# A gate matrix product taken half as seven block products for eight, half plain

## The chip, the cores and the metric

The kernel runs on one NeuronCore of one Trainium2 chip, as one launch. The metric is the device time of the launch in microseconds: 2138.77 us is the median of three runs (2138.43, 2138.77 and 2140.12). Engines are named as in the profile: PE multiplies matrices (TensorE), PEld is its weight load, DVE is VectorE, ACT is ScalarE, POOL is GpSimd, and SP only issues transfers (DMA) between device memory (DRAM) and the on-chip memory SBUF. Matrix products land in a second on-chip memory, PSUM.

## The reference

One layer on 1024 tokens of 2048 channels, all in float32. Only its last part matters here; what comes ahead is unchanged.

```python
hn = rms_norm(h, norm_mix)                     # 2048 channels
q, k, v, gate_a, u, gate_s = split(hn @ w_in)  # attention and SSM groups
y_attn = block_attention(q, k, v) * silu(gate_a)          # 1024 channels
y_ssm = gelu(s5_bidirectional(u, ...))
glu = y_ssm @ w_glu + b_glu
y_ssm = glu[..., :1024] * sigmoid(glu[..., 1024:]) * silu(gate_s)
h = h + concatenate([y_attn, y_ssm]) @ w_out   # 2048 x 2048
gate = sigmoid(rms_norm(h, norm_ple) @ w_ple_gate)        # 2048 x 2048
h = h + gate * (p @ w_ple_proj)                # p has 256 channels
return rms_norm(h, norm_final)
```

## The kernel before

Activations lie with the channel on the 128 partitions and the token on the free axis, so a "k-tile" is 128 input channels and a row tile is 128 output channels; 1024 tokens are two halves of 512. A product keeps float32 accuracy by splitting both operands into a high part H (rounded to `fp32r`) and a rest L, and by three matmuls: H·H, H·L, L·H. A split costs one ACT instruction (the cast, line 310 or 313) and one DVE instruction (the subtraction, line 311 or 314).

The back part of the kernel (function `back`) first runs three product stages of eight units each: stage 0 is `w_glu`, stage 1 the attention half of `w_out`, stage 2 the SSM half of `w_out`. A unit makes two row tiles over all 1024 tokens from eight k-tiles as a 2 by 2 by 2 block product, and needs seven block products for eight (Strassen's scheme in Winograd's form). Each of the seven has 4 k-tiles by 3 matmuls of 128x512, so a unit has 84 matmuls (lines 1183 to 1185). The sums of weight blocks are made as the unit nears (`sw_sum`, on POOL, for units 18 to 22 on DVE); the sums of activation blocks are made once for a stage by `t_make` on POOL and kept in DRAM (`d_t`). The results are combined on DVE as each product leaves PSUM; in `u_out` POOL adds partial results into the residual tile `cx`, and a delayed DVE addition (`close`, line 1273) closes a quarter of it. Stage 2 also squares the new h on ACT and adds up the squares on POOL (line 1285) for the next norm.

The 28 split activation tiles `X` of a stage (7 products by 4 k-tiles, tiles `st`) serve all eight units. They are loaded and split during the last unit of the stage ahead, as their buffers come free: `put` issues the load on SP, `fill` splits the tile some ticks later. A tick comes after every third matmul of a product, and in the product stages fills are left out in one tick of five. With `share=True` every seventh fill is split on POOL instead (lines 318 and 319), 4 of the 28.

The gate stage (`gate`) goes plainly over the two token halves: for each half and each of 16 row tiles it takes all 16 k-tiles of `w_gate` and 2 of `w_proj`, 54 matmuls of 128x512 (lines 1322 to 1324). Its weights pass through three raw buffers (`wraw`), loaded by SP and split on ACT and DVE two tiles ahead of use. `fin_g` scales the gate product by the token's reciprocal root (`xsq`), applies the sigmoid on ACT, multiplies by the second product on DVE, and adds `h` on POOL, which also adds up squares for the final norm. `finish` of the first half (16 DVE instructions, line 1392, and 16 output stores) runs beside the second half.

The order of the work on each engine is the order in which this program is written, with background generators (`bg`) stepped once per tick; each engine, and each DMA queue, works through its own list in order and waits where an operand is not there.

Of the kernel before, what the change touches and what calls it, by code (L numbers as in the profile page):

```python
# [238 lines left out]
class Kernel:  # L239
# [269 lines left out]
    def scratch(self):  # L509
# [15 lines left out]
        self.d_t = [[d(f"d_t{s}_{k}", (2, 128, SEQ)) for k in range(4)] for s in range(3)]  # L525
# [597 lines left out]
    def t_make(self, s, src, four, k_wait, lag):  # L1123

        gp = self.nc.gpsimd

# [185 lines left out]
    def mm_half(self, ps, nk, xs, each=None):  # L1312

        nc = self.nc
        for k in range(nk):
# [9 lines left out]
            if k % 2:  # L1325
                self.tick()
                if each:
                    each(k)

    def h_rstd(self):  # L1330
        for _ in range(3):
            yield
# [4 lines left out]
        for _ in range(4):  # L1337
            yield
# [3 lines left out]
    def fin_g(self, hf, n, pg, pp, ho, hp, acc):  # L1342
# [72 lines left out]
    def put_h(self, hg, hf, ks, wait=4):  # L1415
        for k in ks:
            self.put(hg, k, self.d_h[k][:, self.half(hf)], self.g_ple[:, k : k + 1], wait=wait)

    def gate(self, hf, hg, nhg):
        nc = self.nc  # L1420
        sl = self.half(hf)
        hs, pT = [], {}
        acc = self.t2k(("zz", "t4")[hf])
        self.bg(self.p_load(hf, pT))
        for n in range(16):
# [3 lines left out]
            ho = self.bk.tile([128, 512], F32, name="cx", tag="cx", bufs=4)  # L1429
            nc.sync.dma_start(ho, self.d_h[n][:, sl])  # L1430
            if hf == 0 and n == 0:
                self.bg(self.h_rstd())
            if hf == 0 and 12 <= n < 15:
                self.put_h(nhg, 1, range(3 * n - 36, 3 * n - 33))
            if hf == 0 and n == 15:
                self.mm_half(pg, 16, hg, lambda k: k < 15 and self.put_h(nhg, 1, [9 + k // 2], wait=3))
            else:
                self.mm_half(pg, 16, hg)
# [3 lines left out]
            self.bg(self.fin_g(hf, n, pg, pp, ho, hs[n], acc))  # L1442
        if hf == 1:
            self.drain()
        self.bg(self.finish(hf, hs, acc))

    def back(self, X):
# [8 lines left out]
        units = [(s, u, stages[s][1](u)) for s in range(3) for u in range(8)]
        next(units[0][2])
        nX = {}
        for n, (s, u, thread) in enumerate(units):

            def hook(i):
                if n == 0 and i == 0:
                    self.put_product(X, 6, 0, self.d_y2)
                if u < 7:
                    if u == 6 and i == 6:
                        if s < 2:
                            self.put_product(nX, 0, s + 1, stages[s + 1][0])
# [4 lines left out]
                elif s < 2:
                    if i < 6:
                        self.put_product(nX, i + 1, s + 1, stages[s + 1][0], wait=8, share=True)
                else:
                    if i < 2:
                        if i == 1:
                            self.w_dma()
                            self.w_dma()
                        self.put_h(hg, 0, range(5 + 4 * i, 9 + 4 * i), wait=8)  # L1480
                    elif i == 2:
                        self.put_h(hg, 0, [13], wait=8)
# [12 lines left out]
        self.put_h(hg, 0, [14, 15], wait=3)
        nhg = {}
        self.gate(0, hg, nhg)
        self.gate(1, nhg, None)
# [199 lines left out]
```

## Time and profile before

| | |
|---|---|
| median of three runs | 2138.77 us |
| the profiled execution | 2137.65 us, its span 2135.8 us |
| product stages 0 to 2, first to last matmul | 1227.2 to 1703.9 us |
| gate stage, first to last gate matmul | 1704.6 to 2111.6 us |
| after it, to the end of the span | about 24 us |
| busy share of the span: PE, DVE, ACT, POOL | 97%, 69%, 42%, 43% |

A PE instruction of 128x512 is shown as 0.39 us long, but they are pipelined and overlap, so a busy PE says little; the starts of the matmuls say how fast they pass. Where a table by stretches gives "(x61)", that is the number of instructions that started in the stretch, and with the regular distance between two matmuls it tells how much of the stretch PE lost.

### The profile page before, as it was taken

What the parts mean: (1) busy time and instruction counts of PE and PEld (TensorE: products, weight loads), DVE (VectorE), ACT (ScalarE), POOL (GpSimd) and SP (SyncE); (2) the same over time, 40 slices, a digit from 0 to 9 for tenths busy, and PEclk for the clock granted to TensorE, in tenths of its full rate; (3) what the DMA queues carried; (4) which work ended last, traced back from release to release, by engine and by line L of the source; (5) the groups of instructions that cost most, each with busy time, mean ns of one, the idle gap of its engine ahead of it and who ended that gap; (6) DMA issues with size and microseconds to landing.
All of it is one profiled execution on the core that took longest, in us unless ns stands there. A gap on an engine that the chain in (4) does not pass through costs nothing.

```text
span 2135.8 us, 29630 instructions
## 1 busy us (share of the span) xinstructions
PE 2062.8 (97%) x10140; PEld 1716.9 (80%) x10140; DVE 1469.1 (69%) x2406; ACT 897.7 (42%) x1614; POOL 919.1 (43%) x833
## 2 busy tenths in 40 slices
PE   8999999999999999998999999989999999999996
PEld 6888878888887878887889878878878778888885
DVE  7654787778888787847998976764677743456433
ACT  7111322222222222346777765654565643343332
POOL 0143465555656554613320556477565621221122
PEclk9999999999999999999999999999999999999998
DMA  6333224233233233454421366668765544455433
GB/s 217 91 103 103 78 75 119 74 90 99 83 85 114 73 95 89 148 171 148 159 70 50 128 227 221 217 197 284 250 205 172 176 139 129 130 183 171 150 110 128
DMA packets 183126, 296.50 MB, mean 139 GB/s; under 512 B 28352, under 2 KB 78656, under 8 KB 182720
## 3 DMA queue, kind: packets, MB, share of 16 engines
q1 hardware_dynamic: 181824, 292.51, 43.0%
q10 hardware_dynamic: 1152, 2.10, 0.3%
q8 instruction: 81, 1.33, 0.3%
q14 instruction: 69, 0.57, 0.1%
HBM read 211.37 MB, written 77.92 MB: 135 GB/s over the span
## 4 chain that ended last, share of the span: by engine, by line
PE 54%; DVE 9%; DMA 3%; ACT 2%; issue 1%; POOL 1%; SPq 1%; DVEq 0%; ACTq 0%; POOLq 0%
PE pr L1183 6%; PE pr L1184 6%; PE pr L1185 6%; PE pg L1322 5%; PE pg L1323 5%; PE pg L1324 5%; PE ptr L1015 2%; PE zgs L579 2%; PE zgs L582 2%; PE zgs L580 2%; DMA st<-d_t 1%; PE pv L1029 1%; PE pv L1028 1%; PE pv L1030 1%; PE S L985 1%
## 5 line engine op out<-in xcount | busy, mean ns | idle before, releaser
L311 DVE TENSOR_TENSOR wL<-wraw,wH 128x512 fp32r<-128x512 f32 x304 | 253.5, 852 | 297.5 <-ACT wH L310 294.0
L310 ACT CAST wH<-wraw 128x512 fp32r<-128x512 f32 x304 | 175.5, 595 | 264.5 <-DMA wraw<-in_w_gate_dram 98.5
L1183 PE MATMUL pr<-st,wH 128*128 128x512 f32 x672 | 264.2, 393 | 12.1 <-DVE cx L1273 7.1
L1185 PE MATMUL pr<-st,wL 128*128 128x512 f32 x672 | 263.8, 393 | 0.0
L1184 PE MATMUL pr<-st,wH 128*128 128x512 f32 x672 | 263.4, 392 | 0.2 <-DVE st L311 0.2
L1324 PE MATMUL pg<-st,wL 128*128 128x512 f32 x512 | 200.2, 391 | 3.6 <-DVE wL L311 3.6
L1322 PE MATMUL pg<-st,wH 128*128 128x512 f32 x512 | 200.9, 392 | 1.0 <-ACT wH L310 1.0
L1323 PE MATMUL pg<-st,wH 128*128 128x512 f32 x512 | 200.3, 391 | 0.5 <-DVE st L314 0.5
L1352 POOL TENSOR_TENSOR h<-cx,tz 128x512 f32<-128x512 f32 x31 | 40.9, 1321 | 292.6 <-DVE tz L1350 292.6
L1183 PEld LDWEIGHTS pr<-st,wH 128*128 128x128 f32 x672 | 127.3, 189 | 41.3 <-ACT hp L450 5.8
L897 ACT COPY ks<-kp 16x224 f32<-16x224 f32 x32 | 10.7, 336 | 342.3 <-DVE ks L896 229.3
L1185 PEld LDWEIGHTS pr<-st,wL 128*128 128x128 f32 x672 | 127.3, 189 | 27.7 <-DVE wL L451 0.9
L1184 PEld LDWEIGHTS pr<-st,wH 128*128 128x128 f32 x672 | 127.4, 190 | 26.9 <-DVE st L311 0.6
L1324 PEld LDWEIGHTS pg<-st,wL 128*128 128x128 f32 x512 | 96.5, 188 | 24.8 <-DVE wL L311 4.5
L1322 PEld LDWEIGHTS pg<-st,wH 128*128 128x128 f32 x512 | 96.5, 188 | 23.4 <-ACT wH L310 1.8
L449 ACT CAST wH<-sraw 128x512 fp32r<-128x512 f32 x120 | 74.3, 619 | 96.4 <-PE pr L1184 77.6
L1265 POOL TENSOR_TENSOR cx<-cx,tz 128x512 f32<-128x512 f32 x64 | 87.8, 1384 | 61.1 <-DVE tz L1297 40.7
L1323 PEld LDWEIGHTS pg<-st,wH 128*128 128x128 f32 x512 | 96.5, 188 | 21.5 <-DVE st L314 1.3
L451 DVE TENSOR_TENSOR wL<-sraw,hp 128x512 fp32r<-128x512 f32 x120 | 81.9, 683 | 42.3 <-ACT hp L450 36.4
L770 POOL TENSOR_TENSOR tab<-pa 128x512 f32<-128x512 f32 x32 | 41.4, 1293 | 157.8 <-DVE r L905 157.8
L579 PE MATMUL zga<-hH,wH 128*128 128x512 f32 x256 | 104.0, 406 | 0.0
L579 PE MATMUL zq<-hH,wH 128*128 128x512 f32 x256 | 103.3, 404 | 0.0
(377 smaller groups left out, 5556.5 us busy)
## 6 DMA issues: line engine op xcount, KB each, us to landing
wraw<-in_w_in_dram SPq DMA_DIRECT2D x144, 256.0 KB
wraw<-in_w_gate_dram SPq DMA_DIRECT2D x128, 256.0 KB
sraw<-in_w_out_dram SPq DMA_DIRECT2D x64, 256.0 KB
st<-d_t SPq DMA_DIRECT2D x48, 256.0 KB
sraw<-in_w_glu_dram SPq DMA_DIRECT2D x32, 256.0 KB
cx<-in_xT_dram SPq DMA_DIRECT2D x16, 512.0 KB
d_p<-cx SPq DMA_DIRECT2D x16, 512.0 KB
cx<-d_p SPq DMA_DIRECT2D x16, 512.0 KB
```

The lines of the kernel that those rows point to most:

```text
L310: nc.scalar.copy(H, src)
L311: nc.vector.tensor_tensor(L, src, H.bitcast(F32), ALU.subtract)
L449: self.nc.scalar.copy(H, raw)
L451: self.nc.vector.tensor_tensor(L, raw, hp, ALU.subtract)
L579: nc.tensor.matmul(ps[h], H[:, kk, :], rH[:, s], start=(k == 0), stop=False)
L1183: nc.tensor.matmul(ps, H[:, k], x[0], start=(k == 0), stop=False)
L1184: nc.tensor.matmul(ps, H[:, k], x[1], start=False, stop=False)
L1185: nc.tensor.matmul(ps, L[:, k], x[0], start=False, stop=(k == 3))
L1265: nc.gpsimd.tensor_tensor(x[:, h], x[:, h], u, ALU.add)
L1322: nc.tensor.matmul(ps, H[:, k % 4], x[0], start=(k == 0), stop=False)
L1323: nc.tensor.matmul(ps, H[:, k % 4], x[1], start=False, stop=False)
L1324: nc.tensor.matmul(ps, L[:, k % 4], x[0], start=False, stop=(k == nk - 1))
```

## The change

The gate's k-tiles 0 to 7 become a fourth product stage of eight units (stage 3): two row tiles per unit over all tokens, seven block products for eight. Its activation blocks are h times the norm's gain: `t_make` gets the gain and applies it on ACT before POOL makes the sums; products 0, 1 and 5 take the gain as they are split. The partial sums are stored to DRAM (`d_g`, 16 tiles of 512 KB). The gate stage then takes only k-tiles 8 to 15, loads `d_g` beside `h` (one row tile ahead), and `fin_g` has one more DVE instruction, which adds the partial sum. The token's reciprocal root (`h_rstd`) is made during stage 3. `share` is no longer passed at any stage, so POOL splits no fills in stages 0 to 2 any more.

```diff
@@ w_plan, sw_plan: the weights
-                tile_(self.i["w_gate"][n], 16)
+                tile_(self.i["w_gate"][n][:, 1024:], 8)
                 tile_(self.i["w_proj"][n], 2)
...
             (self.i["w_out"], [(2 * m, 2 * m + 1) for m in range(8)], 8),
+            (self.i["w_gate"], [(2 * m, 2 * m + 1) for m in range(8)], 0),
@@ t_make
+        for _ in range(13 if gain is not None else 0):
+            yield
...
             for _ in range(k_wait):
                 yield
+            if gain is not None:
+                for i in range(2):
+                    kt = k + 4 * i
+                    self.nc.scalar.activation(two[i][0], two[i][0], AF.Copy, scale=gain[:, kt : kt + 1])
+                yield
+                yield
             gp.tensor_tensor(b[0], b[1], b[0], ALU.subtract)
@@ put_product
+            if s == 3 and i in (0, 1, 5):
+                kt = k + 4 * (i > 0)
+                kw["gain"] = self.g_ple[:, kt : kt + 1]
             self.put(X, (i, k), a, **kw)
@@ new: u_gate (two row tiles r, seven products)
+        ps = yield
+        u1 = self.t2k("tz")
+        nc.scalar.copy(u1, ps)
+        ps = yield
+        nc.vector.tensor_tensor(r[0][:, h0], ps, u1, ALU.add)
+        ps = yield
+        nc.vector.tensor_tensor(u1, ps, u1, ALU.add)
+        ps = yield
+        u2 = self.t2k("tz")
+        nc.vector.tensor_tensor(u2, ps, u1, ALU.add)
+        ps = yield
+        nc.vector.tensor_tensor(u1, ps, u1, ALU.add)
+        nc.vector.tensor_tensor(r[1][:, h1], ps, u2, ALU.add)
+        ps = yield
+        nc.vector.tensor_tensor(r[0][:, h1], ps, u1, ALU.add)
+        self.bg(self.later(8, (self.d_g[2 * m], r[0])))
+        ps = yield
+        nc.vector.tensor_tensor(r[1][:, h0], ps, u2, ALU.add)
+        self.bg(self.later(8, (self.d_g[2 * m + 1], r[1])))
@@ fin_g
-        nc.vector.tensor_tensor(t, pg, self.xsq[:, self.half(hf)], ALU.mult)
+        nc.vector.tensor_tensor(t, pg, gp, ALU.add)
+        nc.vector.tensor_tensor(t, t, self.xsq[:, self.half(hf)], ALU.mult)
@@ gate
+        def load(n):
+            x = self.bk.tile([128, 2, 512], F32, name="cx", tag="cx", bufs=4)
+            nc.sync.dma_start(x[:, 0], self.d_h[n][:, sl])
+            nc.sync.dma_start(x[:, 1], self.d_g[n][:, sl])
+            return x
...
+            if hf == 0 and n == 13:
+                self.put_h(nxt[0], 1, range(8, 16))
+            y = load(n + 1) if n < 15 else None
+            self.mm_half(pg, 8, hg)
@@ back
+            (self.d_h, self.u_gate),
...
-                            self.put_h(hg, 0, range(5))
-                elif s < 2:
+                            self.put_h(hg, 0, range(8, 13))
+                elif s < 3:
                     if i < 6:
-                        self.put_product(nX, i + 1, s + 1, stages[s + 1][0], wait=8, share=True)
+                        self.put_product(nX, i + 1, s + 1, stages[s + 1][0], wait=8)
...
+            elif u == 3 and s == 2:
+                self.bg(self.t_make(3, self.d_h, self.four_sm, 12, 6, self.g_ple))
+            elif u == 1 and s == 3:
+                self.bg(self.h_rstd())
```

What this moves on the engines, at three places. First, the transition from stage 0 to stage 1 on DVE, before; `st<-st` are fills, `tz<-pr` takes a product out of PSUM, `wL<-sraw,hp` makes a weight's rest:

```order
L1219 TENSOR_TENSOR tz<-pr,tz 128x512
L451 TENSOR_TENSOR wL<-sraw,hp 128x512
L311 TENSOR_TENSOR st<-st 128x512 x2
L1222 TENSOR_TENSOR tz<-pr,tz 128x512
L451 TENSOR_TENSOR wL<-sraw,hp 128x512
L311 TENSOR_TENSOR st<-st 128x512 x3
```

And the same place on DVE in the changed kernel:

```order
L1232 TENSOR_TENSOR tz<-pr,tz 128x512
L452 TENSOR_TENSOR wL<-sraw,hp 128x512
L311 TENSOR_TENSOR st<-st 128x512 x3
L1235 TENSOR_TENSOR tz<-pr,tz 128x512
L452 TENSOR_TENSOR wL<-sraw,hp 128x512
L311 TENSOR_TENSOR st<-st 128x512 x3
```

Where two fills stood between two PSUM reads, three stand now; so it is at four places in this transition and four in the next.

Second, the end of stage 2 on DVE, before: the last fills of the gate's activations, then the gate's first weight rests (`wL<-wraw,wH`) between the closing additions (`cx<-pr,cx`):

```order
L314 SCALAR_TENSOR_TENSOR st<-st,vec 128x512 x3
L1301 TENSOR_TENSOR tz<-pr,tz 128x512
L314 SCALAR_TENSOR_TENSOR st<-st,vec 128x512 x2
L1273 TENSOR_TENSOR cx<-pr,cx 128x512
L311 TENSOR_TENSOR wL<-wraw,wH 128x512 x2
L1273 TENSOR_TENSOR cx<-pr,cx 128x512 x2
L311 TENSOR_TENSOR wL<-wraw,wH 128x512 x2
```

And DVE in the changed kernel, from the last closing additions of stage 2 into the first unit of stage 3 (`cx<-pr,tz` is `u_gate`):

```order
L311 TENSOR_TENSOR st<-st 128x512
L452 TENSOR_TENSOR wL<-sraw,hp 128x512
L311 TENSOR_TENSOR st<-st 128x512 x2
L1286 TENSOR_TENSOR cx<-pr,cx 128x512
L314 SCALAR_TENSOR_TENSOR st<-st,vec 128x512
L452 TENSOR_TENSOR wL<-wraw,hp 128x512
L314 SCALAR_TENSOR_TENSOR st<-st,vec 128x512 x3
L1333 TENSOR_TENSOR cx<-pr,tz 128x512
L452 TENSOR_TENSOR wL<-sraw,hp 128x512
L311 TENSOR_TENSOR st<-st 128x512 x3
L1335 TENSOR_TENSOR tz<-pr,tz 128x512
```

This place now has the shape of the other two transitions, 28 fills instead of 16, mixed with weight rests and PSUM reads.

Third, the start of the gate stage on SP, before (`pT` is p, `cx<-d_h` is the h that `fin_g` adds):

```order
L1196 DMA d_h_192<-cx 128x1024
L1196 DMA d_h_193<-cx 128x1024
L1098 DMA st<-d_h_192 128x512
L1098 DMA st<-d_h_193 128x512
L1430 DMA cx<-d_h_178 128x512
L387 DMA wraw<-in_w_gate_dram 128x512
L387 DMA wraw<-in_w_proj_dram 128x256
L1405 DMA cx<-in_pT_dram 128x512 x2
L387 DMA wraw<-in_w_gate_dram 128x512 x4
```

And SP at the start of the gate stage in the changed kernel:

```order
L387 DMA wraw<-in_w_proj_dram 128x256
L1209 DMA d_g_223<-cx 128x1024
L1442 DMA cx<-in_pT_dram 128x512 x2
L1209 DMA d_g_224<-cx 128x1024
L1209 DMA d_g_225<-cx 128x1024
L1464 DMA cx<-d_h_178 128x512
L1465 DMA cx<-d_g_210 128x512
L1464 DMA cx<-d_h_179 128x512
L1465 DMA cx<-d_g_211 128x512
L387 DMA wraw<-in_w_gate_dram 128x512 x2
```

The last two activation loads and their wait for the last stores of h are gone; behind the last stores of `d_g` now stand four loads into `cx` ahead of the weights of the second row tile.

## Rows read from the trace of the kernel before

**Rows 1.** The page, busy time: us, share of the span, instructions.

```profile
PE 2062.8 (97%) x10140; PEld 1716.9 (80%) x10140; DVE 1469.1 (69%) x2406; ACT 897.7 (42%) x1614; POOL 919.1 (43%) x833
```

**Rows 2.** Timeline of PE in a regular stretch: start, length.

```profile
1329.67 0.39 PE L1183 MATMUL pr<-st,wH 128*128 128x512 f32 x1
...
1341.91 0.39 PE L1183 MATMUL pr<-st,wH 128*128 128x512 f32 x1
```

**Rows 3.** Instructions on `pr` and `pg`: ns min/median/max, first and last start.

```profile
L1183 PE MATMUL pr<-st,wH x672: 387/389/711, 1227.3 to 1703.4; 128*128 128x512 f32 x168
...
L1322 PE MATMUL pg<-st,wH x512: 387/389/791, 1704.6 to 2111.2; 128*128 128x512 f32 x171
```

**Rows 4.** Stretches: length, then PE, PEld, DVE, ACT, POOL, clock, DMA share, GB/s.

```profile
1385.00:1405.00 20.00, 14.09 (x53) 10.38 (x52) 19.90 (x25) 14.87 (x28) 12.19 (x9) 0.91 0.62 220
1424.00:1444.00 20.00, 20.00 (x90) 16.55 (x89) 9.89 (x15) 8.83 (x15) 18.29 (x15) 1.00 0.71 233
1523.00:1543.00 20.00, 20.00 (x90) 16.55 (x89) 15.00 (x21) 15.08 (x27) 11.42 (x9) 1.00 0.78 266
1543.00:1563.00 20.00, 15.64 (x61) 12.16 (x60) 20.00 (x22) 12.70 (x23) 17.66 (x13) 0.91 0.87 301
1623.00:1643.00 20.00, 20.00 (x90) 16.57 (x89) 14.46 (x19) 11.97 (x21) 11.87 (x9) 1.00 0.48 158
1683.00:1704.00 21.00, 21.00 (x94) 17.28 (x93) 18.00 (x22) 17.22 (x30) 14.23 (x11) 1.00 0.56 190
1704.00:1717.00 13.00, 9.00 (x39) 6.99 (x37) 7.55 (x10) 3.51 (x7) 6.58 (x5) 0.87 0.40 132
1717.00:1753.00 36.00, 33.70 (x141) 25.32 (x142) 16.19 (x36) 15.96 (x27) 3.87 (x3) 1.00 0.47 143
1753.00:1803.00 50.00, 50.00 (x221) 41.20 (x220) 20.64 (x29) 16.41 (x29) 10.34 (x8) 1.00 0.38 119
```

**Rows 5.** Timeline of PE after two waits and at the broadcast.

```profile
1395.53 0.63 PE L1183 MATMUL pr<-st,wH 128*128 128x512 f32 x1
...
1709.02 0.79 PE L1324 MATMUL pg<-st,wL 128*128 128x512 f32 x1 [3.65 <-DVE wL L311]
...
1727.97 1.98 PE L358 MATMUL bc<-tq,ones 128*128 128x512 f32 x4 [1.15 <-DVE tq L352]
```

**Rows 6.** PE instructions by line from 1290 us on: the column sums.

```profile
L345 PE MATMUL cs<-ones,xsq 128*128 128x1 f32 x16 | 1.8, 245 | 0.0
```

**Rows 7.** By line, 1523 to 1565 us: count, busy us, mean ns.

```profile
L311 DVE TENSOR_TENSOR st<-st 128x512 fp32r<-128x512 f32 x23 | 25.0, 1129 | 0.0
...
L319 POOL TENSOR_TENSOR st<-st 128x512 fp32r<-128x512 f32 x4 | 6.3, 1583 | 0.3
L318 POOL CAST st<-st 128x512 fp32r<-128x512 f32 x4 | 3.7, 925 | 0.6 <-PE pr L1184 0.6
```

**Rows 8.** Line 311, its fills in the whole run.

```profile
L311 DVE TENSOR_TENSOR st<-st x64: 676/690/1790, 1221.9 to 1565.1; 128x512 fp32r<-128x512 f32 x64
```

**Rows 9.** By line, gate stage, 1753 to 1903 us.

```profile
L311 DVE TENSOR_TENSOR wL<-wraw,wH 128x512 fp32r<-128x512 f32 x50 | 42.8, 856 | 76.9 <-ACT wH L310 76.9
L1345 DVE TENSOR_TENSOR tz<-pg,xsq 128x512 f32<-128x512 f32 x13 | 8.9, 683 | 0.0
L1350 DVE TENSOR_TENSOR tz<-pp,tz 128x512 f32<-128x512 f32 x12 | 8.3, 693 | 8.4 <-ACT tz L1346 8.4
...
L311 DVE TENSOR_TENSOR wL<-wraw,wH 128x256 fp32r<-128x256 f32 x12 | 4.9, 411 | 0.0
...
L1352 POOL TENSOR_TENSOR h<-cx,tz 128x512 f32<-128x512 f32 x12 | 15.5, 1292 | 107.4 <-DVE tz L1350 107.4
```

**Rows 10.** By line, second half of the gate stage, 1903 to 1953 us.

```profile
L1392 DVE SCALAR_TENSOR_TENSOR h<-h,vec,zz 128x512 f32<-128x512 f32 x8 | 5.9, 743 | 0.3 <-ACT zz L1386 0.3
```

**Rows 11.** Timeline of SP and ACT: weight loads, and the cast that waits.

```profile
1803.73 7.23 SPq L387 DMA_DIRECT2D wraw<-in_w_gate_dram  x4
...
1812.81 0.62 ACT L310 CAST wH<-wraw 128x512 fp32r<-128x512 f32 x1 [2.93 <-DMA wraw<-in_w_gate_dram]
```

More of the change, by code (lines that the diff above doesn't have):

```diff
@@ L524, in scratch @@
         self.d_h = [d(f"d_h{n}") for n in range(KD)]
-        self.d_t = [[d(f"d_t{s}_{k}", (2, 128, SEQ)) for k in range(4)] for s in range(3)]
+        self.d_t = [[d(f"d_t{s}_{k}", (2, 128, SEQ)) for k in range(4)] for s in range(4)]
+        self.d_g = [d(f"d_g{n}") for n in range(KD)]
         self.d_pa = d("d_pa", (128, NG, NPA))
@@ L1121, in y_prep, with t_make @@
             nc.sync.dma_start(self.d_y2[j][:, 512:1024], t[:, 0:512])
-    def t_make(self, s, src, four, k_wait, lag):
+    def t_make(self, s, src, four, k_wait, lag, gain=None):
         gp = self.nc.gpsimd
+        for _ in range(13 if gain is not None else 0):
+            yield
         def src_parts(a, n):
@@ L1310, in u_out, with u_gate, mm_half @@
         yield
-    def mm_half(self, ps, nk, xs, each=None):
+    def u_gate(self, m):
+        nc = self.nc
+        h0, h1 = self.half(0), self.half(1)
+        r = [self.bk.tile([128, SEQ], F32, name="cx", tag="cx", bufs=4) for _ in range(2)]
+        ps = yield
[17 more added lines that the diff above has]
+        self.bg(self.later(8, (self.d_g[2 * m + 1], r[1])))
+        yield
+    def mm_half(self, ps, nk, xs):
         nc = self.nc
@@ L1326, in mm_half @@
                 self.tick()
-                if each:
-                    each(k)
     def h_rstd(self):
-        for _ in range(3):
+        for _ in range(8):
             yield
@@ L1336, in h_rstd @@
         dg = [self.spread(self.rk[:, 4 * h : 4 * h + 4]) for h in range(2)]
-        for _ in range(4):
+        for _ in range(10):
             yield
@@ L1340, in h_rstd, with fin_g @@
             self.nc.scalar.copy(self.xsq[:, self.half(h)], self.rows(dg[h]))
-    def fin_g(self, hf, n, pg, pp, ho, hp, acc):
+    def fin_g(self, hf, n, pg, pp, ho, gp, hp, acc):
         nc = self.nc
         t = self.t2k("tz")
-        nc.vector.tensor_tensor(t, pg, self.xsq[:, self.half(hf)], ALU.mult)
+        nc.vector.tensor_tensor(t, pg, gp, ALU.add)
+        nc.vector.tensor_tensor(t, t, self.xsq[:, self.half(hf)], ALU.mult)
         nc.scalar.activation(t, t, AF.Sigmoid)
@@ L1416, in put_h, with gate @@
         for k in ks:
-            self.put(hg, k, self.d_h[k][:, self.half(hf)], self.g_ple[:, k : k + 1], wait=wait)
-    def gate(self, hf, hg, nhg):
+            self.put(hg, k - 8, self.d_h[k][:, self.half(hf)], self.g_ple[:, k : k + 1], wait=wait)
+    def gate(self, hf, hg, pT, nxt):
         nc = self.nc
         sl = self.half(hf)
-        hs, pT = [], {}
+        hs = []
         acc = self.t2k(("zz", "t4")[hf])
-        self.bg(self.p_load(hf, pT))
+        def load(n):
[3 more added lines that the diff above has]
+            return x
+        x = load(0)
         for n in range(16):
@@ L1428, in gate @@
             pg = self.psC("pg")
[L1429 to L1438, printed above, removed]
+            if hf == 0 and n == 13:
+                self.put_h(nxt[0], 1, range(8, 16))
+            y = load(n + 1) if n < 15 else None
+            self.mm_half(pg, 8, hg)
             pp = self.psC("pp")
@@ L1441, in gate @@
             hs.append(hp[:, n % 2])
-            self.bg(self.fin_g(hf, n, pg, pp, ho, hs[n], acc))
-        if hf == 1:
+            self.bg(self.fin_g(hf, n, pg, pp, x[:, 0], x[:, 1], hs[n], acc))
+            x = y
+        if hf == 0:
+            self.bg(self.p_load(1, nxt[1]))
+        else:
             self.drain()
@@ L1452, in back @@
             (self.d_ms, lambda m: self.u_out(m, self.d_p, self.d_h, True)),
+            (self.d_h, self.u_gate),
         ]
-        hg = {}
+        hg, pT = {}, {}
         self.paced = True
-        units = [(s, u, stages[s][1](u)) for s in range(3) for u in range(8)]
+        units = [(s, u, stages[s][1](u)) for s in range(4) for u in range(8)]
         next(units[0][2])
@@ L1465, in hook @@
                     if u == 6 and i == 6:
-                        if s < 2:
+                        if s < 3:
                             self.put_product(nX, 0, s + 1, stages[s + 1][0])
@@ L1470, in hook @@
                             self.w_dma()
-                            self.put_h(hg, 0, range(5))
-                elif s < 2:
+                            self.put_h(hg, 0, range(8, 13))
+                elif s < 3:
                     if i < 6:
-                        self.put_product(nX, i + 1, s + 1, stages[s + 1][0], wait=8, share=True)
+                        self.put_product(nX, i + 1, s + 1, stages[s + 1][0], wait=8)
                 else:
[L1476 to L1482, printed above, removed]
+                    if i == 0:
+                        self.put_h(hg, 0, range(13, 16), wait=8)
+                    elif i == 1:
+                        self.w_dma()
+                        self.w_dma()
                     elif i == 5:
@@ L1491, in back @@
                 X, nX = nX, {}
-        self.paced = False
         while self.bgs:
             self.tick()
[L1495 to L1498, printed above, removed]
+        self.paced = False
+        nxt = ({}, {})
+        self.gate(0, hg, pT, nxt)
+        self.gate(1, *nxt, None)
     COL = {"q": 0, "k": 8, "v": 10, "ga": 12, "u": 20, "gs": 28}
```

1 line of the change is left out of this document (added).

## The prediction

> **What bounds the kernel now.** I read the busy shares first: PE 97%, DVE 69% [rows 1]. A busy PE says little here, so next come its starts. Eighteen triples take 1341.91 - 1329.67 = 12.24 us, 0.2267 us for each of 54 matmuls [rows 2], though each is shown as 0.39 us [rows 3]. The product stages run from 1227.3 to 1703.9 us and the gate from 1704.6 to 2111 us [rows 3]. A stretch of W us with n PE instructions loses W - 0.2267 n. Read so, the stretches [rows 4] show three places of loss. The change from stage 0 to 1 loses 20 - 53 x 0.2267 = 8.0 us, with another 1.3 us in the 19 us behind it, 9.3 in all. The change from stage 1 to 2 (1543 to 1563) loses 6.2 us. The start of the gate loses 1704 to 1753 us: 180 instructions, of which 20 are column sums and the broadcast; 49 - 160 x 0.2267 = 12.7 us, less about 3.7 us of those 20 [rows 5, 6], leaves 9 us. Elsewhere nothing is lost (1424, 1523, 1623, 1683, 1753) [rows 4]. So PE sets the end everywhere but at these three places; there DVE is busy 19.90 and 20.00 of 20 us [rows 4], and at the gate's start PE waits 3.65 us for a weight rest that DVE has queued behind fills [rows 5]. Behind such a wait PE runs at half clock for a while: 0.63 us a matmul in place of 0.39, granted clock 0.91 over the stretch, the 1.2 GHz level for some 3 us [rows 4, 5].
>
> **The change part by part.** *Matmuls.* The gate loses 16 x 2 x 8 x 3 = 768 matmuls and stage 3 adds 8 x 84 = 672. 96 fewer at 0.2267 us: -21.8 us, on PE and so on the path.
>
> *The old gate start.* Its 9 us came from the last two h tiles (stored, reloaded and split after the last unit), from fills ahead of weight rests on DVE, and from the broadcast's 1.15 us wait [rows 5]. Now the gate's eight tiles are old by then, only eight are split, and the norm's sums and broadcast move into stage 3 with ten ticks between them. -9 us; the 3.7 us of work stay.
>
> *A new transition, stage 2 to 3.* The last unit of stage 2 before has 14 of 16 fills and DVE at 18.0 of 21 us without loss [rows 4]. Now it has 28, and stage 3 behind it with its weight rests: the shape of 1 to 2, which costs 6.2 us with 24 fills on DVE. Four more, and twelve with gain, add some 3 us of DVE; against that `u_gate` empties PSUM at once (no three ticks of delay, no POOL add to wait for), and no residual is loaded. I take +7, near that row. Ends: 0, if the earlier emptying hides the backlog, and 14, the 9.3 us of 0 to 1 plus four fills at 1.13 us [rows 7].
>
> *POOL's fills back on DVE and ACT.* Eight in all, at the two old transitions. A DVE fill takes 0.69 us at the median, 0.68 at least and 1.79 at most [rows 8]; around 1 to 2 the mean is 1.129 [rows 7]. So 23 fills lose 23 x 0.44 = 10 us, while POOL is busy 11.42 + 17.66 = 29 us [rows 4], a third of a us for each POOL us. The four POOL splits take 6.3 + 3.7 = 10 us [rows 7]. Taking them away returns some 3.4 us to DVE; four fills more cost 2.8 to 4.5. I take 0. Ends: -8, if both transitions lose half of what they cost, +12, if nothing returns and each stays four fills and a half-clock spell longer.
>
> The Trainium skill, "SBUF — State Buffer", section "Who interferes with whom", says that a VectorE instruction with two SBUF inputs and a GpSimd instruction that reads SBUF hold a shared port pair in turn, the whole instruction long. The stretched fills [rows 7, 8] agree; but the third of a us for each POOL us says that a large part of POOL's time meets DVE while it reads PSUM or waits, which the rule alone would not tell.
>
> *`t_make` in stage 2.* 16 POOL instructions and 8 ACT gains over units 3 to 6, four per 23 ticks (23 x 0.68 = 15.6 us). POOL there is at 11.87 of 20 us [rows 4], 9.3 in 15.6; four at 1.29 [rows 9] make it 14.5, or 93%. In stage 1 the same generator runs with POOL at 18.29 of 20 and nothing lost [rows 4]. But in stage 2 POOL also waits for squares, and DVE's closing additions wait for POOL's: if it slips, PSUM isn't emptied. +2; ends 0 and 7 (all of it at the contended 1.58 [rows 7], 1.7 us over for four periods).
>
> *Stage 3 itself.* Seven PSUM reads and seven weight rests, about 10 us of DVE in 19: no loss.
>
> *The gate's start.* The weights of the second row tile stand on SP behind the loads into `cx`, and these behind the stores of the last `d_g`. From the last matmul T of stage 3: addition 0.7, store 3.5, the second pair of `cx` 1.5 (512 KB at 301/0.87 = 346 GB/s [rows 4]), weight tile 2 (issue ended at 1810.96, cast begun at 1812.81 [rows 11]), cast and rest 1.3: T + 9, wanted at T + 6.8. +2; ends 0 and 7 (the p splits stand ahead of the last addition on DVE, and a half-clock spell).
>
> *The gate's row tiles.* 30 matmuls make 6.80 us, 54 made 12.24. DVE per row tile now: two weight rests at 0.856, one at 0.411, the new addition from PSUM 0.68, the scaling now from SBUF 0.69, the product 0.693, and 0.7 idle for the sigmoid [rows 8, 9]: 4.9 of 6.80, where 5.9 of 12.24 were used. In the second half the first half's 16 output instructions at 0.743 [rows 10] come in 32 ticks of 1.36 us, or 6.4 row tiles: +1.9, so 6.8 of 6.8, entered with a lag from the eight fills of row tiles 13 to 15. Two tiles of splitting ahead cover some 4 us. +4; ends 0 and 14.
>
> *The end.* One more DVE instruction ahead of the last sigmoid: +0.6.
>
> Sum: -21.8 - 9 + 7 + 0 + 2 + 2 + 4 + 0.6 = -15.2 us. The profiled execution took 2137.65 us (span 2135.8), so 2122.4; the median of the runs shown lies 1.1 us above it, so 2123.5, say 2123 us.
>
> **The rivals.**
>
> *All transitions clean.* With POOL out of the fills and PSUM emptied earlier, the new transition costs 2 and the old ones lose 3 less each, the gate 1: 2123 - 5 - 6 - 5 = 2107 to 2110 us. For it: the mean of 1.129 against 0.69. Against it: DVE has no idle time there to begin with.
>
> *Fills overload DVE, and the kernel is slower.* At each of three transitions DVE is the bound, and every fill it gets takes the contended 1.13 us: 0 to 1 and 1 to 2 grow by 4.5 us and a further half-clock spell of 1.5, +12; 2 to 3 costs 9.3 + 4.5 + 1.5 = 15.3 where I took 7, +8. 2123 + 20 = 2143 to 2145 us. It decides from the point where the transitions together cost over 15 + 7 us more than now, some 37 us where they cost 15.5. For it: DVE is full there [rows 4]; against it, POOL gives back its share.
>
> *The lock binds the gate.* If each of POOL's two 1.29 us additions per row tile [rows 9] held DVE for its whole length, DVE would need 4.9 less the 0.33 us of stretch already in it, plus 2.6: 7.1 us per row tile, and 9.0 beside the outputs. 0.3 x 26 + 2.2 x 6.4 = 22 us where I took 4: 2141 us, no change. The skill's section named above would give this, read by itself; the trace gives 50 x 0.166 = 8.3 us of stretch for 24 such additions, 31 us [rows 8, 9], a quarter.
>
> *Something runs late in a stage.* POOL slips in stage 2 (+7 for +2), or in the second half the weight ring, with three buffers, turns too slowly: 2 us to land, 1.5 to split, 1.1 to issue, 1.5 for the `cx` pair, 1.9 for 640 KB of output in a row tile: 8 of 6.8 us, for 6.4 row tiles another 8. 2128 to 2135 us.
>
> *It does nothing for PE.* It would if the gate were bound by transfers; PE's 221 instructions in 50 us [rows 4] exclude that for before.
>
> **How the numbers follow.** My forecast 0.55, clean transitions 0.20, something late 0.10, lock 0.07, overload 0.08. The measurement tells 0.2%, 4.3 us, from no change, so faster is below 2134.5 and slower above 2143: faster 0.85, no change 0.07, slower 0.08. The range is 2107 to 2138: it takes in the clean case at its edge and the late cases, and leaves out the lock and the overload. The forecast's own range is 2113 to 2132.
>
> **What would show it.** 96 matmuls fewer at the same 0.2267 us. The first gate matmul some 155 us after the first of stage 3 (8 x 19.04 and little else). DVE full around the start of stage 3, PE waiting there on a closing addition, 7 us lost, and 9 and 6 at the old transitions as before. No wait of 1 us or more in the row tiles of the first half of the gate; in the second half waits for `wL` or `wH` in its first seven row tiles, about 4 us. I am wrong if the gate stage takes over 230 us (217.6 in matmuls), if PE waits in units 3 to 6 of stage 2, or if the old transitions change by more than 3 us each.

## The result, and the profile after

The changed kernel takes 2170.6 us (median of 4 runs, 2169.62 to 2170.86), the kernel before 2139.14 us beside it: ratio 1.0148, 95% interval 1.0137 to 1.016. It is 31 us slower where 15 us faster was forecast. The profiled spans are 2167.6 and 2135.8 us.

Busy shares of the changed kernel's page, to be held against [rows 1]:

```profile
PE 2057.5 (95%) x10044; PEld 1697.1 (78%) x10044; DVE 1531.0 (71%) x2506; ACT 946.5 (44%) x1698; POOL 963.4 (44%) x865
```

The 96 matmuls are gone, and PE's share fell with them: PE now waits. The table by stretches says where (columns as in [rows 4]):

```profile
1385.00:1405.00 20.00, 16.28 (x60) 11.48 (x59) 19.90 (x29) 16.76 (x31) 3.85 (x3) 0.91 0.61 216
1405.00:1425.00 20.00, 20.00 (x90) 16.46 (x89) 11.75 (x19) 8.76 (x16) 17.09 (x14) 1.00 0.66 214
1543.00:1565.00 22.00, 18.58 (x80) 14.47 (x80) 21.41 (x32) 16.05 (x30) 8.83 (x7) 1.00 0.82 276
1690.00:1722.00 32.00, 22.33 (x91) 17.75 (x90) 31.50 (x37) 24.12 (x44) 18.46 (x13) 0.89 0.79 291
1722.00:1730.00 8.00, 6.38 (x28) 4.65 (x26) 8.00 (x10) 6.27 (x12) 3.73 (x3) 1.00 0.17 53
1752.00:1869.70 117.70, 117.70 (x521) 97.44 (x520) 63.46 (x95) 58.97 (x100) 27.26 (x21) 1.00 0.39 125
1869.70:1880.00 10.30, 7.20 (x32) 5.60 (x30) 1.71 (x4) 0.43 (x1) 0.00 (x0) 1.00 0.70 239
1880.00:1980.00 100.00, 94.79 (x393) 73.74 (x394) 56.20 (x80) 36.55 (x68) 32.31 (x25) 0.98 0.51 163
1980.00:2030.00 50.00, 37.61 (x142) 28.29 (x143) 27.59 (x49) 20.34 (x35) 10.66 (x8) 0.90 0.48 153
2030.00:2142.00 112.00, 100.41 (x405) 75.28 (x404) 64.54 (x95) 39.12 (x72) 35.65 (x28) 0.98 0.52 164
```

Width less 0.2267 times the count is what PE lost. The old transition 0 to 1 (first two rows) loses 6.0 us, 1 to 2 loses 3.9; the new one (rows four and five) 11.4 + 1.7. Counted by units, the last of stage 2 and the first of stage 3 take 52.4 us (1680.58 to 1733.01) where their 168 matmuls need 38.1, so 14.3 us are lost there. From 1752 to 1869.7 stage 3 loses nothing. Unit 6 of stage 2 (counted from 0), just ahead of the new transition, takes 20.6 us (1659.96 to 1680.58) where 84 matmuls need 19.0; nearly all of that is one wait for a closing addition:

```profile
1664.17 0.47 PE L1196 MATMUL pr<-st,wH 128*128 128x512 f32 x1 [1.33 <-DVE cx L1286]
```

The gate loses 3.0 us at its start, then 10.9, 17.8 and 20.2 us. Its matmuls run for 271 us where 960 of them need 217.6:

```profile
L1360 PE MATMUL pg<-st,wH x256: 387/389/795, 1869.9 to 2140.4; 128*128 128x512 f32 x128
```

The transitions can be set against the kernel before, the gate's first 100 us can't: no engine is full there. DVE is busy 56.2 us, ACT 36.6, POOL 32.3, and yet PE stands still in each row tile. PE's waits from 1870 to 2141 us (total, times, longest):

```profile
PE pg L1360 <- ACT wH L310: 16.6, 12, 3.3
PE pg L1362 <- DVE wL L311: 10.9, 20, 0.7
PE pp L1360 <- ACT sraw L310: 4.5, 1, 4.5
```

Weights, then, whose cast and rest come late. Why engines that idle are late is read from one row tile. Timeline of ACT in the changed kernel (start, length, and in brackets the idle time before it and what ended it):

```profile
1938.59 0.63 ACT L1399 ACTIVATE tq<-h 128x512 f32<-128x512 f32 x1 [2.13 <-POOL h L1389]
1939.12 1.43 ACT L310 CAST wH<-wraw 128x512 fp32r<-128x512 f32 x3
1943.43 0.63 ACT L1383 ACTIVATE tz<-tz 128x512 f32<-128x512 f32 x1 [2.88 <-DVE tz L1382]
1946.19 0.63 ACT L1399 ACTIVATE tq<-h 128x512 f32<-128x512 f32 x1 [2.13 <-POOL h L1389]
```

DVE in the same row tile:

```profile
1939.76 2.31 DVE L311 TENSOR_TENSOR wL<-wraw,wH 128x512 fp32r<-128x512 f32 x3 [2.58 <-ACT wH L310]
1941.99 0.68 DVE L1381 TENSOR_TENSOR tz<-pg,cx 128x512 f32<-128x512 f32 x1
1942.70 0.69 DVE L1382 TENSOR_TENSOR tz<-tz,xsq 128x512 f32<-128x512 f32 x1
1944.09 0.69 DVE L1387 TENSOR_TENSOR tz<-pp,tz 128x512 f32<-128x512 f32 x1 [0.70 <-ACT tz L1383]
```

and POOL:

```profile
1944.86 1.30 POOL L1389 TENSOR_TENSOR h<-cx,tz 128x512 f32<-128x512 f32 x1 [4.28 <-DVE tz L1387]
```

Follow the starts: square 1938.59 (ACT), casts 1939.12 (ACT), three rests 1939.76 (DVE), new addition 1941.99, scaling 1942.70, sigmoid 1943.43 (ACT), product 1944.09 (DVE), h 1944.86 (POOL), next square 1946.19 (ACT). That is a closed ring of 7.60 us. On ACT the casts stand *behind* the square, and the square waits for this row tile's last result; on DVE the next row tile's first instruction stands *behind* the rests, which wait for those casts. Each engine works for a part of the ring and then waits for its turn. The ring was there before as well, with one DVE instruction less, but 54 matmuls took 12.24 us [rows 2] and covered it. 30 matmuls take 6.80 us and do not. Splitting the weights two tiles ahead does not help, since the ring sets the time at which they are split.

### The profile page after: what moved, and what is told of

It reads as the page before. It is cut to its first block, busy times and chain, and to the rows that moved or that the text cites. A ratio compares the mean times of both kernels' runs of the same rounds, so it can differ in the third digit from the quotient of the medians.

```text
span 2167.6 us, 29832 instructions
## 1 busy us (share of the span) xinstructions
PE 2057.5 (95%) x10044; PEld 1697.1 (78%) x10044; DVE 1531.0 (71%) x2506; ACT 946.5 (44%) x1698; POOL 963.4 (44%) x865
## 4 chain that ended last, share of the span: by engine, by line
PE 45%; DVE 10%; DMA 6%; issue 3%; ACT 3%; POOL 2%; SPq 1%; DVEq 0%; ACTq 0%; POOLq 0%
PE pr L1196 7%; PE pr L1197 7%; PE pr L1198 7%; PE zgs L581 2%; PE zgs L584 2%; PE zgs L582 2%; PE ptr L1017 2%; DVE wL L311 2%; DMA wraw<-in_w_proj_dram 1%; PE zq L581 1%; PE zq L584 1%; PE zq L582 1%; DMA wraw<-in_w_gate_dram 1%; PE pv L1031 1%; PE pv L1030 1%
## 5 line engine op out<-in xcount | busy, mean ns | idle before, releaser
L1196 PE MATMUL pr<-st,wH 128*128 128x512 f32 x896 | 351.9, 393 | 19.7 <-DVE cx L1286 10.3
L1198 PE MATMUL pr<-st,wL 128*128 128x512 f32 x896 | 350.5, 391 | 1.8 <-DVE wL L452 1.8
L1197 PE MATMUL pr<-st,wH 128*128 128x512 f32 x896 | 350.1, 391 | 0.2 <-DVE st L311 0.2
L311 DVE TENSOR_TENSOR wL<-wraw,wH 128x512 fp32r<-128x512 f32 (+1 forms) x240 | 207.2, 886 | 201.7 <-ACT wH L310 200.3
L1196 PEld LDWEIGHTS pr<-st,wH 128*128 128x128 f32 x896 | 168.8, 188 | 60.3 <-issue 13.5
L310 ACT CAST wH<-wraw 128x512 fp32r<-128x512 f32 (+1 forms) x240 | 135.6, 587 | 160.0 <-PE zu L582 55.9
L1198 PEld LDWEIGHTS pr<-st,wL 128*128 128x128 f32 x896 | 169.0, 189 | 39.6 <-DVE wL L452 4.4
L1197 PEld LDWEIGHTS pr<-st,wH 128*128 128x128 f32 x896 | 169.0, 189 | 35.5 <-DVE st L311 0.6
L451 ACT COPY hp<-wH 128x512 f32<-128x512 f32 x224 | 132.4, 591 | 10.5 <-DVE wL L452 3.5
L1360 PE MATMUL pg<-st,wH 128*128 128x512 f32 x256 | 104.4, 408 | 16.8 <-ACT wH L310 16.6
L1362 PE MATMUL pg<-st,wL 128*128 128x512 f32 x256 | 105.2, 411 | 11.1 <-DVE wL L311 10.9
L581 PE MATMUL zgs<-hH,wH 128*128 128x512 f32 x256 | 102.8, 401 | 0.4 <-ACT wH L310 0.4
L1361 PE MATMUL pg<-st,wH 128*128 128x512 f32 x256 | 102.1, 399 | 0.0
```

The lines of the kernel that those rows point to most:

```text
L310: nc.scalar.copy(H, src)
L311: nc.vector.tensor_tensor(L, src, H.bitcast(F32), ALU.subtract)
L451: self.nc.scalar.copy(hp, H.bitcast(F32))
L581: nc.tensor.matmul(ps[h], H[:, kk, :], rH[:, s], start=(k == 0), stop=False)
L1196: nc.tensor.matmul(ps, H[:, k], x[0], start=(k == 0), stop=False)
L1197: nc.tensor.matmul(ps, H[:, k], x[1], start=False, stop=False)
```

## The experiments

Each line is a median beside the kernel before on the same chip (2139.4 to 2140.0 us there), with the ratio's 95% interval. The changed kernel was timed only in the section above, so what an edit gives back is counted from its 2170.6 us. A row tile's period is the distance from one start of the new addition to the next.

**The ring: put the square later.** In `fin_g`:

```diff
-        yield
+        for _ in range(3):
+            yield
         if n == 0:
             nc.scalar.activation(acc, hp, AF.Square)
```

> The changed kernel with one edit: the square of a finished row tile (and POOL's addition of it) is written two ticks later, so that ACT has the cast of the next row tile's first weights ahead of it. No engine gets less work and no transfer changes. Theory A (a closed ring of in-order waits: cast of the next weights behind the square on ACT, the square behind POOL's addition, that behind the sigmoid and three DVE instructions, these behind the weight rests, these behind the casts; 7.6 us round): the ring opens, a row tile falls from 7.6 to 6.8 to 7.0 us, the gate stage from 271 to 225 to 235 us, the whole to 2126 to 2136 us. Rival B (weights land late because d_g is loaded on the same queue): no change, 2168 to 2172 us. Rival C (DVE with POOL's port waits is full): no change either.

2154.4 us (2147.0 to 2160.5), ratio 1.0067 (1.0044 to 1.009). 16 us back, but the period fell only to 7.38. The square still stood ahead of the second weight tile's cast, so the ring closed again through it, one weight rest shorter. The direction is the ring's; the size was missed, because three steps did not take the square out of it.

**The transfers: no load of the partial sums.** The load of `d_g` is taken out, and `fin_g` adds h in its place, so the partial sums are left out of the result.

```diff
-            nc.sync.dma_start(x[:, 1], self.d_g[n][:, sl])
```

> The changed kernel without the 32 loads of d_g (8.4 MB); the partial sum is left out, h stands in its place in the same DVE addition. Theory A (ring of waits): the loads are no link of the ring, the first half keeps its 7.6 us a row tile; 2165 to 2171 us. Rival B (weights late behind d_g on the queue): row tiles fall towards 6.8 us in both halves, 2140 us or less. Rival C: no change.

2168.0 us, ratio 1.0128 (1.0108 to 1.0148), period 7.61 as before. 8 MB less to load change the time by 2.6 us, and the period not at all. These loads are not what holds the row tiles.

**A shorter link: h added on DVE.** POOL's addition in the ring takes 1.30 us, DVE's 0.7.

```diff
-        eng = nc.vector if last else nc.gpsimd
+        eng = nc.vector
         eng.tensor_tensor(hp, ho, t, ALU.add)
```

> The changed kernel with the addition of h on DVE instead of POOL for every row tile. Theory A: the ring's link of 1.3 us on POOL becomes one of 0.6 to 0.7 on DVE, a row tile falls from 7.6 to about 6.9 us, the whole by some 20 us to 2145 to 2155 us. Rival B (weights late): no change, 2168 to 2172. Rival C (DVE full): 0.6 us more DVE work for a row tile, 2171 to 2190 us.

2153.1 us, ratio 1.0067 (1.0041 to 1.0093), period 7.09. More work on DVE, the engine with the most, and the kernel gets 17 us faster. A full DVE would have made it slower, so DVE's amount of work is not what sets the period.

**The part without the block products: the kernel before, `share` not passed.**

```diff
-wait=8, share=True)
+wait=8)
```

> The kernel before with one part of the change alone: share is not passed, so the eight fills that POOL split at the two stage transitions go to ACT and DVE. Theory (POOL's instructions hold up DVE's fills, so taking its splits away returns more than four fills cost): the transitions lose 3 and 2.5 us less as in the changed kernel's trace, 2132 to 2135 us. Rival (the fills cost DVE what POOL gives back, as the prediction had it): 2137 to 2140 us.

2133.6 us, ratio 0.9975 (0.9962 to 0.9987): this part alone makes the kernel *before* some 5 to 6 us faster. Its three stretches, from an execution of 2130.3 us:

```profile
1385.00:1405.00 20.00, 16.71 (x70) 12.51 (x69) 19.90 (x30) 14.62 (x27) 3.95 (x3) 1.00 0.73 243
1405.00:1425.00 20.00, 20.00 (x89) 16.48 (x89) 10.47 (x17) 9.29 (x16) 17.62 (x15) 1.00 0.67 218
1543.00:1565.00 22.00, 19.09 (x78) 15.63 (x78) 20.12 (x31) 14.79 (x28) 8.75 (x7) 0.92 0.72 245
```

The last two stretches in the kernel before, which [rows 4] cuts otherwise:

```profile
1405.00:1425.00 20.00, 20.00 (x83) 16.34 (x82) 11.57 (x19) 8.21 (x14) 14.06 (x12) 0.91 0.62 191
1543.00:1565.00 22.00, 17.64 (x70) 13.78 (x68) 22.00 (x25) 12.70 (x23) 17.66 (x13) 0.92 0.87 299
```

POOL does 4 us in the first where it did 12, and the 70 matmuls are 17 more than before in the same 20 us [rows 4]. DVE starts 30 instructions in 19.90 busy us where it started 25: the same time, more done in it. The granted clock in the first 40 us is 1.00 where it was 0.91. By the count of starts the two transitions lose 9.2 and 6.1 us in the kernel before, 4.0 and 4.3 here, and 6.0 and 3.9 in the changed kernel.

**The square behind all casts.** As the first experiment, with `range(4)`.

> The changed kernel with the square written three ticks later, behind both casts of the next row tile on ACT (in e1 it stood behind the first only, and the ring closed again at 7.38 us). Theory A (ring of in-order waits): what is left of the ring goes by the cast of the next w_proj tile and its rest ahead of the addition on DVE, some 5.5 us, under the 6.80 us of 30 matmuls; row tiles of the first half at 6.80 us, those beside the outputs below 8; gate stage 228 to 238 us, the whole 2130 to 2142 us on a chip where the kernel before takes 2140. Rival C (DVE with POOL's port waits needs over 7 us a row tile whatever the order): row tiles stay at 7.3 to 7.4 us.

2143.5 us, ratio 1.0019 (1.0008 to 1.003): 27 of the 31 us. The gate's matmuls run for 242 us in place of 271, and in its first twelve row tiles the period is 6.61 to 6.98 us, PE's own pace. ACT now takes the casts ahead of the square:

```profile
1932.93 0.63 ACT L1383 ACTIVATE tz<-tz 128x512 f32<-128x512 f32 x1 [1.95 <-DVE tz L1382]
1933.47 0.60 ACT L310 CAST wH<-wraw 128x512 fp32r<-128x512 f32 x1
1934.72 0.62 ACT L310 CAST wH<-wraw 128x512 fp32r<-128x512 f32 x1 [0.64 <-PE pg L1361]
1936.07 0.63 ACT L1400 ACTIVATE tq<-h 128x512 f32<-128x512 f32 x1 [0.73 <-POOL h L1389]
```

and the cast that waits here waits for PE to free a weight buffer, so PE sets the pace. One number in one line, an order and no work, is what nearly the whole loss hung on.

**The control: the same edit in the kernel before.**

> The kernel before with the same later square. Theory A: there 54 matmuls, 12.24 us, cover the ring's length (it would take some 8 to 9 us with five weight rests), so nothing is gained: within 2 us of the kernel before. Rival (the square's place on ACT costs something by itself in any gate): 10 us or more less.

2139.4 us, ratio 0.9997 (0.9987 to 1.0007): nothing, as it must be where the ring is covered by 12.24 us of matmuls.

**What is left, one loss after the other.** Each of the next two adds one edit to the version before it.

```diff
-        eng = self.nc.vector if 18 <= u < 23 else self.nc.gpsimd
+        eng = self.nc.vector if 18 <= u < 25 else self.nc.gpsimd
```

> e5, and the weight sums of units 23 and 24 on DVE instead of POOL. Theory (around the start of stage 3 each POOL instruction holds back one of DVE's fills for its whole length: 3 fills took 4.8 and 5.1 us there): DVE gets four sums of 0.7 us more for a unit but its fills fall to 0.7 to 0.8 us; the wait of 8.3 us at the last closing additions of stage 2 falls below 4, 4 to 8 us less than e5. Rival (DVE is full with its own work): no gain, or a loss of 2 to 5 us.

2139.6 us, ratio 0.9996 (0.9984 to 1.0009), 4 us below the version before it. In the changed kernel the new transition reads so on DVE:

```profile
1701.03 4.79 DVE L311 TENSOR_TENSOR st<-st 128x512 fp32r<-128x512 f32 x3
1705.74 0.68 DVE L1314 TENSOR_TENSOR tz<-pr,tz 128x512 f32<-128x512 f32 x1
1706.34 0.67 DVE L452 TENSOR_TENSOR wL<-sraw,hp 128x512 fp32r<-128x512 f32 x1
1706.93 5.12 DVE L311 TENSOR_TENSOR st<-st 128x512 fp32r<-128x512 f32 x3
1711.98 0.68 DVE L1286 TENSOR_TENSOR cx<-pr,cx 128x512 f32<-128x512 f32 x1
```

and so on POOL:

```profile
1706.91 1.26 POOL L1278 TENSOR_TENSOR cx<-cx,tz 128x512 f32<-128x512 f32 x1
1708.13 1.71 POOL L438 TENSOR_TENSOR sraw<-sraw 128x512 f32<-128x512 f32 x1
1709.80 1.71 POOL L438 TENSOR_TENSOR sraw<-sraw,wraw 128x512 f32<-128x512 f32 x1
```

Three fills take 4.79 and 5.12 us, while POOL works beside them without a pause, on residual additions and weight sums; the reads of PSUM between them keep their 0.68. The last row on DVE is the closing addition for which PE waits 8.3 us. With the sums of units 23 and 24 on DVE as well, DVE has more to do, and both groups of three fills take 1.88 us. The last version below shows the same place with the same time:

```profile
1707.24 1.38 DVE L438 TENSOR_TENSOR sraw<-sraw 128x512 f32<-128x512 f32 x1
1708.54 1.88 DVE L311 TENSOR_TENSOR st<-st 128x512 fp32r<-128x512 f32 x3
1710.35 0.68 DVE L1286 TENSOR_TENSOR cx<-pr,cx 128x512 f32<-128x512 f32 x1
```

The wait fell only to 6.2 us, since the sums now stand in DVE's own list.

The second edit loads the second half's two raw `p` tiles at row tile 12 of the first half, not at its end:

```diff
+            if hf == 0 and n == 12:
+                self.praw = self.p_raw()
```

> e6, and the raw p of the second half loaded into a buffer of its own during row tile 12 of the first half, so that its loads don't wait on SP for cx buffers nor hold x and weights of the second half back there. Theory: the single wait of PE for sraw (4 to 5 us at the first row tile of the second half) goes, and a wait for the weights behind it: 4 to 7 us less than e6. Rival (what comes next, the weights' ring, is late at that place anyway): 0 to 2 us less.

2137.9 us, ratio 0.9987 (0.9975 to 1.0). The wait for the split `p` fell from 3.8 to 1.5 us, the time by under 2, which the two intervals don't separate from nothing. That is what the rival expected: what comes next is late at that place as well.

**Three bursts in the gate**, each added to the version above by itself. First, the factor of the first half's output goes to PSUM, so that the 16 output multiplies read one operand from SBUF in place of two:

```diff
+        if hf == 0:
+            acc = self.psA("rp")[:, 0:512]
         nc.scalar.copy(acc, r)
```

> Kernel: e7_and_p_early (2137.9 us, span 2135.9) with one more edit: the factor that finish(0) multiplies the finished first half by is kept in a PSUM tile, so the 16 scalar_tensor_tensor of the outputs read one operand from SBUF instead of two. In e7 the row tiles beside the outputs take 7.7 to 8.6 us instead of 6.8, some 11 us in eight rows, and the output multiply lasted 0.74 us alone but 1.78 us where a GpSimd add ran beside it (15 of them in 60 us, mean 1.09). Theory L (two-SBUF-operand VectorE instructions wait for GpSimd's): the multiplies fall to about 0.75 each, so 15 x 0.34 = 5 us less of VectorE, rows of 7.2 to 7.8, time 2131 to 2135. Rival M (the stretch only moves on to the weight rests L311, which still read two SBUF operands and are stretched the same way whenever a GpSimd add starts beside them): the output multiply's mean falls to 0.75, the mean of L311 rises from 1.12 by as much, rows stay 8 us, time 2136 to 2139. Rival D (VectorE's plain share of output work): as M in the time, with both means unchanged.

2133.6 us, ratio 0.9973 (0.996 to 0.9986). DVE by line, 2000 to 2060 us (count, busy us, mean ns), without the edit:

```profile
L311 DVE TENSOR_TENSOR wL<-wraw,wH 128x512 fp32r<-128x512 f32 x15 | 16.8, 1119 | 1.1 <-PE pp L1362 0.9 <-ACT wH L310 0.2
L1430 DVE SCALAR_TENSOR_TENSOR h<-h,vec,zz 128x512 f32<-128x512 f32 x15 | 16.4, 1091 | 1.8 <-ACT zz L1424 1.8
L311 DVE TENSOR_TENSOR wL<-wraw,wH 128x256 fp32r<-128x256 f32 x8 | 4.2, 524 | 0.1
```

and with it:

```profile
L311 DVE TENSOR_TENSOR wL<-wraw,wH 128x512 fp32r<-128x512 f32 x16 | 15.3, 955 | 3.8 <-ACT wH L310 3.8
L1432 DVE SCALAR_TENSOR_TENSOR h<-h,vec,rp 128x512 f32<-128x512 f32 x16 | 11.8, 738 | 1.7 <-ACT rp L1426 1.7
L311 DVE TENSOR_TENSOR wL<-wraw,wH 128x256 fp32r<-128x256 f32 x9 | 6.6, 734 | 0.5 <-ACT wH L310 0.2
```

The multiply fell from 1091 to 738 ns (at most 748, where it had been up to 1810). Of the stretch some moved on to the small rests (524 to 734 ns), as rival M had it, but not to the large ones (1119 to 955): 37.4 us for 38 instructions became 33.7 us for 41. The time is 3 us lower by the ratios, whose intervals overlap, so the price of this stretch is shown by the trace and not by the time. The Trainium skill, "SBUF — State Buffer", section "Who interferes with whom", says that a VectorE instruction with at most one SBUF input does not contend with GpSimd (outside certain modes); the 738 ns agree.

Second, the second half's eight h tiles are queued two a row tile from row tile 11 on:

```diff
-            if hf == 0 and n == 13:
-                self.put_h(nxt[0], 1, range(8, 16))
+            if hf == 0 and n > 10:
+                a = 8 + 2 * (n - 11)
+                self.put_h(nxt[0], 1, range(a, min(a + 2, 16)))
```

> Kernel: e7_and_p_early (2137.9 us) with one more edit: the eight loads and fills of the second half's h tiles are queued two per row tile from row tile 11 on, instead of eight at once at row tile 13. In e7 the rows there take 12.1 and 9.7 us instead of 6.8 (8.2 us together), and ScalarE waits for raw weights that stand on SP's queue behind the eight loads. Theory B (burst: eight fills in eight steps and eight 256 KB loads ahead of the weights): rows 11 to 16 at 7.0 to 7.6, time 2131 to 2134. Rival T (only the total VectorE work counts: 4.9 us a row plus 8 fills of 0.74 to 1.8): the 8 us come back as 1 to 2 us in each of five rows, time 2136 to 2139.

2130.2 us, ratio 0.9956 (0.9939 to 0.9972). Without it, the worst wait there was ACT's for a raw weight tile, behind the eight loads:

```profile
1973.06 0.62 ACT L310 CAST wH<-wraw 128x512 fp32r<-128x512 f32 x1 [5.61 <-DMA wraw<-in_w_gate_dram]
```

With it the periods of 12.1 and 9.7 us give way to six of 6.8 to 8.2. Part of the work comes back there, as rival T had it, but the time fell by as much as B expected and a little more. The burst cost that time; how much of it was the loads ahead of the weights and how much the eight fills in a row was not taken apart.

Third, the output multiplies come one in four steps, not one in two:

```diff
-                yield
-                yield
+                for _ in range(4):
+                    yield
```

> Kernel: e7_and_p_early (2137.9 us) with one more edit: the 16 output multiplies of the first half are issued one in four steps instead of one in two (1.25 a row tile instead of 2.5). Theory D (VectorE is full there: 4.9 us of its own row work + 2.5 x 0.74 to 1.8): rows fall to 6.8 to 7.3, about 8 us less, time 2128 to 2132. Rival R (what lengthens these rows is the output stores on SP's queue ahead of the weights, or the ring of waits and not the multiplies): the same bytes and waits remain, rows of 7.6 to 8.4 over twice as many row tiles, time 2137 to 2142.

2132.5 us, ratio 0.9964 (0.9953 to 0.9976). From the third on, row tiles beside the outputs take 7.0 to 7.8 us where most took 7.7 to 8.5, and there are more of them. The time lies just above D's range and 4.5 us below R's; the row tiles lie between the two, so spreading the multiplies gave most of what D expected and not all.

**All three.**

> Kernel: e7_and_p_early (2137.9 us) with the three edits of e9, e10 and e11 together. If the three losses are separate and as priced: 2120 to 2127, so below the kernel before (2139) and below the kernel before without the shared fills (2133.6). If VectorE's total work in the gate is the limit: 2133 to 2138. Theory: the block products' saved matmuls can only show once the row tiles run at TensorE's own 6.8 us, which needs each of these bursts out of the way; what is left then is the third transition (about 12 us) and the gate's start (3.7 us).

2126.0 us (2121.5 to 2127.1), ratio 0.9932 (0.9914 to 0.995), within the range for separate losses: faster than the kernel before, and further below it (13 us by medians, 15 by the ratio) than the kernel before without `share` is (6 and 5 us), so that some 7 to 9 us come from the block products and their repairs. Of the repairs only the later square was tried in the kernel before; its gate had little for the others to win, as its 1572 matmuls from 1753 us on took 3.5 us more than 1572 x 0.2267. The new transition and three stretches of the gate:

```profile
1690.00:1722.00 32.00, 25.52 (x105) 20.67 (x104) 30.73 (x42) 25.32 (x45) 11.31 (x10) 0.89 0.88 314
1880.00:1950.00 70.00, 70.00 (x303) 57.23 (x303) 42.89 (x64) 28.98 (x52) 27.97 (x19) 0.98 0.58 185
1980.00:2030.00 50.00, 47.96 (x205) 38.51 (x204) 38.82 (x58) 23.05 (x42) 18.36 (x12) 0.97 0.56 175
2030.00:2100.00 70.00, 69.25 (x303) 56.40 (x301) 54.48 (x72) 27.10 (x51) 29.02 (x20) 1.00 0.61 199
```

The third row now has 205 matmuls in 50 us where the changed kernel had 142; the gate's matmuls run for 228.7 us. DVE is busier than in the changed kernel and PE waits less. By their ratios against e7's 0.9987 the three edits won 11.8 us together and 3.0 + 6.6 + 4.9 = 14.5 us one by one; the difference lies within the intervals, so whether they share a wait is open. Left are the new transition (32 - 105 x 0.2267 = 8.2 us in the first row) and some 3.5 us at the gate's start; nothing more was tried on these.

## Why the prediction was wrong

- **The gate's row tiles, +4 (0 to 14), is the step that failed.** It measured +49 (10.9 + 17.8 + 20.2). It summed DVE's time for a row tile, 4.2 us busy and 0.7 idle of 6.80, and as a sum that was right (56.2 us in 100, or 4.3 a row tile): no engine is full. What it left out is that a row tile passes DVE, ACT, DVE, POOL and ACT in turn, and that the next weights stand behind the last of these on ACT's list. The 0.7 us of idle time for the sigmoid was taken as the only wait of the chain; the 1.30 us of POOL, the square and the casts were in it too. e5 and e8 show it from both sides: 27 us back by order alone, nothing where the matmuls cover the ring. The order took the gate's matmuls from 271 to 242 us; the later edits, above all the three on bursts, took them to 228.7. The prediction named the fills and the outputs too, but priced the outputs by DVE's busy time and the fills only as a lag.
- **In the second half, part of it is of the kind that the lock rival named.** Once the ring was open, rows beside the outputs took 7.4 to 8.5 us; with an operand in PSUM the multiply there fell from 1091 to 738 ns. The rival's 22 us, and its claim that this alone decides, did not come.
- **The new transition, +7 (0 to 14), measured 14.3.** Mis-sized: six of the fills there took 1.6 to 1.7 us each beside POOL's additions, not the 1.13 of the row that it was taken from. e6 got 4 us back by this; what makes up the rest is open.
- **`t_make` in stage 2, +2 (0 to 7), measured 1.6, but not by POOL.** The one wait of unit 6 goes back to ACT: there the second gain of `t_make` waits 1.86 us for its load of h (1654.99 us), a weight's cast stands behind it in ACT's list, DVE waits 4.1 us for that weight, and the closing addition comes late. The size was right by luck; it is the same kind of miss as in the gate.
- **Removing `share`, 0 (-8 to +12), measured -5.4** (3.2 and 2.2) in the changed kernel and -5 to -6 alone (e4). The price of a POOL us to DVE was taken as a third of a us; in these stretches more came back.
- **The gate's start, +2, measured 3.0. The end, +0.6, measured 2.6** (26.8 us behind the last gate matmul, 24.2 before): besides the new addition, the last scaling took 1.41 us beside a POOL addition.
- **The matmuls, -21.8, and the old gate's start, -9, held**; the column sums and the broadcast cost 3.6 us in the second unit of stage 3, as the prediction kept for them. The sum of what was measured is -21.8 - 9 - 5.4 + 14.3 + 1.6 + 3 + 49 + 2.6 = +34 us, against 31.8 between the two spans; the kernel before lost some 3 us in its gate rows too, which the prediction took as nothing.
- Its own tests spoke: "over 230 us" in the gate (271), a wait of PE in units 3 to 6 of stage 2 (1.33 us), and the first of the old transitions, which moved by 3.2 us (the bound was 3; the second moved by 2.2). The rivals didn't hold the case: the only slower one put the loss into fills.

## What to carry to other kernels

When a change shortens a loop's matmuls, follow one iteration through all in-order engines until it meets itself again, and compare that round with the new matmul time; busy shares did not show it here. If the round is longer, first move what waits for the end of an iteration (here a square) behind what the next iteration needs (here the weight casts). Then spread bursts of loads, fills and outputs over the iterations, since a short loop has no slack to take them.

## What was not expected of the hardware

- A DVE instruction of 128x512 with two SBUF operands took 0.69 to 0.74 us alone and up to 1.6 to 1.8 us beside GpSimd instructions (three in a row 4.79 and 5.12 us); with an operand in PSUM it stayed at 0.68 to 0.75 us in the same stretches. Moving GpSimd's sums to the busier DVE made three fills 1.88 us, and the kernel 4 us faster.
